# A decoder layer's projection with an interleaved paged attention: both pages' scores moved into one run, and gathered keys turned in place

## The chip, the cores and the metric

The kernel runs on one core of a Trainium2 chip. The metric is the device time of one execution in microseconds. Three runs of the kernel before gave 2318.6, 2320.21 and 2324.48 us, median 2320.21. TensorE is called PE, VectorE DVE, ScalarE ACT, GpSimd POOL and SyncE SP, as in the profile; PEld is PE's loading of weights.

## The reference

One layer is computed for a prompt of 2048 tokens and for a sample group of 8 sequences with 4 new tokens each. A normalised input is multiplied by one wide matrix (the projection); its columns feed four groups (a convolution module, a pooling mixer, stick-breaking attention, attention to memory tokens), whose gated outputs go through a second matrix. The part that the change touches is the sample group's stick-breaking attention over 8192 cached positions, kept in pages of 128 positions that a table of page numbers names:

```python
k_past = cache_k[l][page_table].reshape(bs, past, SB_HEADS, SB_HEAD_DIM)
v_past = cache_v[l][page_table].reshape(bs, past, SB_HEADS, SB_HEAD_DIM)

def sb_block(q, k, v, bias, q_pos, k_pos):
    z = (jnp.einsum('nqhd,nkhd->nhqk', q, k).astype(jnp.float32) * (SB_HEAD_DIM ** -0.5)
         + bias.astype(jnp.float32)[None, :, None, None])
    mask = (k_pos[None, :] < q_pos[:, None])[None, None]
    log_beta = jax.nn.log_sigmoid(z)
    log_1m = jnp.where(mask, jax.nn.log_sigmoid(-z), 0.0)
    rc = lax.cumsum(log_1m, axis=3, reverse=True)
    a = jnp.exp(jnp.where(mask, log_beta + rc - log_1m, -jnp.inf))
    return jnp.einsum('nhqk,nkhd->nqhd', a.astype(v.dtype), v)
```

Scores become a weight and a running product from the last position backwards, so the pages of a sequence are taken from the last to the first; the weights then sum the cached values.

## The kernel before

**The projection.** For each block of 128 output columns, `mm3` multiplies 24 pairs (high and low parts of weights and inputs) of 384, 288 or 512 token columns into one of two PSUM tiles (`z_tile`, a ring of two), called here a group. After 12 matmuls and again after the group's end it hands control back. `z_evac` then empties the tile: ACT for some column blocks, ACT's sigmoid and a multiplication on DVE for the gates (kinds cg, sg, pg, mg; names sg.. and gmg), DVE and ACT for the memory queries (mq). Tasks advance one step at each hand-back: attention to memory tokens (ms, mpt, my), the depthwise convolution on DVE (cacc, groups of two multiply-adds), transposes, stores.

**The sample part** is written as a generator, `sample_stages`, which is advanced when a running sum of the projection's work passes one; between two `yield`s stands what is issued at one hand-back. It has N = 64 stages: 2 groups of 4 sequences, 32 pairs of pages each. In a stage n:

- `load_k(n, ml)` issues on POOL one indirect gather of 128 rows of 8 KB (one page of keys for four sequences) into a tile kt; `load_v(n)` issues four gathers of 128 rows of 4 KB into tiles vt;
- `turn(n, ml)` transposes the keys of page ml in 32 by 32 blocks on DVE, in two halves of 128x1024;
- `scores(n, ml)` runs 16 fp32 products (32 matmuls in the trace) with a stationary tile of 32 columns into columns 128 ml on of the PSUM tile sSA;
- `weights(n)` takes two sigmoids of the scores (ACT; sgam and sbe), the running product (DVE scan sE) and the product sbe;
- `transposes(n)` transposes sbe on PE into the other half of sSA, ACT copies it to saT;
- `values(n)` adds the value sums of the pair, 8 fp32 products (16 matmuls in the trace), into sO, also with 32 columns.

Before the change a stage has four steps: the first page's scores and the second page's turn; the transposes of stage n - 1; the second page's scores with the value sums of n - 1, the value gathers of n, the weights of n and the first page's turn of n + 1; a step without work. Gathered keys lie in a ring of two tiles kt (`KT`), and the turned ones in one tile T (`TB`), so a turn waits until PE has read the keys turned before; each turn is followed by the gather of the next stage's page of the same parity.

**What sets the order.** The steps are put among the projection's work by `main`'s loop, and the program's framework then lays out each engine's instructions by its own planning: an instruction of DVE can stand earlier or later than in the source. Each engine works off its own row in order; PE, DVE and POOL meet at semaphores.

## Time and profile before

| | |
|---|---|
| median of three runs | 2320.21 us |
| profiled execution | 2319.3 us |
| its span | 2317.6 us |
| PE, DVE, ACT, POOL busy | 2244.9, 1704.7, 1081.0, 1261.0 us |
| granted PE clock, mean | 0.993 |
| turns on DVE (L990) | 256, 308.6 us |
| gathers of keys, of values (L957) | 128 and 256, 128.7 and 252.7 us of POOL |
| scores (L1003), value sums (L1042) | 4096 and 1024 matmuls |

The page divides the span among engines; matmul ends are modelled, so the starts of matmuls, not PE's busy share, tell how closely they follow. Waits are given as who waited for whom, with the sum, the number and the longest. The sample part's scores run from 152.7 to 1427.1 us of the span, all of it under the projection.

### The profile page before, as it was taken

Reading aid. Unit: us, or ns where it says so; the run is one execution under the profiler, and the core shown is the slowest. Engines: PE = TensorE matmul, PEld = TensorE weight load, DVE = VectorE, ACT = ScalarE, POOL = GpSimd, SP = SyncE. Lnnn points to the kernel's source line nnn. Section 1 sums busy time; section 2 is a strip of 40 time slices with the busy share of each in tenths; the row PEclk is TensorE's granted clock in tenths of the full one; section 3 lists DMA queues with packets and bytes.
Section 4 is the critical chain, followed back from the end, with each engine's and each line's share of the span. In section 5 each row is a group of like instructions: output and inputs, shape, how many; then the busy total and the mean of one; then the engine's idle time right before and its main releaser. Section 6 shows DMA issues by size and latency. Waiting matters only on the chain. (4 is left out here: it accounts for less than half of the span.)

```text
span 2317.6 us, 43407 instructions
## 1 busy us (share of the span) xinstructions
PE 2244.9 (97%) x16512; PEld 1812.9 (78%) x16512; DVE 1704.7 (74%) x2334; ACT 1081.0 (47%) x1977; POOL 1261.0 (54%) x1375
## 2 busy tenths in 40 slices
PE   7999999999999999999999999999999999999997
PEld 7998888898888777777777777667677667788775
DVE  5343786969756755378777768899989885686997
ACT  5332343242442322234233234588879875454553
POOL 3554545556464555555545455489999973620002
PEclk9999999999999999999999999999999999999999
DMA  6689977878778899987977885666554307876774
GB/s 206 208 291 316 336 259 255 286 256 277 255 252 301 306 358 338 345 284 255 319 260 259 278 275 178 160 173 192 160 161 129 98 15 217 285 236 194 251 261 152
DMA packets 338188, 558.32 MB, mean 241 GB/s; under 512 B 29162, under 2 KB 213610, under 8 KB 321580
## 3 DMA queue, kind: packets, MB, share of 16 engines
q1 hardware_dynamic: 282604, 286.83, 39.9%
q0 software_dynamic: 55376, 268.72, 32.8%
q8 instruction: 130, 2.13, 0.4%
q14 instruction: 78, 0.64, 0.1%
HBM read 465.35 MB, written 90.72 MB: 240 GB/s over the span
## 5 line engine op out<-in xcount | busy, mean ns | idle before, releaser
L990 DVE STREAM_TRANSPOSE T<-kt 128x1024 f32<-128x1024 f32 x256 | 308.6, 1226 | 183.1 <-PE sSA L1003 174.8
L957 POOL DMA_INDIRECT vt<-in_cache_v_dram,idv x256 | 252.7, 987 | 255.1 <-PE sO L1042 194.2
L642 DVE SCALAR_TENSOR_TENSOR cacc<-U,par,cacc 128x512 f32<-128x512 f32 x480 | 359.9, 750 | 11.0
L1384 POOL TENSOR_TENSOR be<-be,E 128x512 f32<-128x512 f32 (+4 forms) x316 | 311.9, 999 | 18.0 <-DVE E L1375 12.4
L957 POOL DMA_INDIRECT kt<-in_cache_k_dram,idk x128 | 128.7, 1005 | 200.2 <-DVE T L990 156.0
L1375 DVE TENSOR_TENSOR_SCAN E<-gam,cr,ZM 128x513 f32<-128x513 f32 x192 | 230.6, 1260 | 3.7 <-POOL csq L1499 1.0
L2032 PE MATMUL acc<-wohi,mh 128*128 128x512 f32 (+1 forms) x480 | 192.4, 401 | 0.0
L2032 PE MATMUL acc<-wolo,mh 128*128 128x512 f32 (+1 forms) x480 | 188.7, 393 | 0.0
L2032 PE MATMUL acc<-wohi,ml 128*128 128x512 f32 x448 | 176.9, 395 | 4.7 <-DVE ml L1767 4.7
L1405 ACT COPY at<-AT 128x512 f32<-128x512 f32 (+1 forms) x288 | 153.5, 592 | 47.9 <-PE AT L1403 42.9
L1403 PE MATMUL AT<-ident,be 128*128 128x128 f32 x1082 | 153.3, 281 | 14.6 <-ACT at L1405 10.9
L1403 PEld LDWEIGHTS AT<-ident,be 128*128 128x128 f32 x1082 | 121.2, 143 | 55.0 <-issue 22.8
L1303 ACT ACTIVATE be<-S 128x1024 f32<-128x1024 f32 (+1 forms) x158 | 153.8, 974 | 6.7 <-PE S L1298 4.1
L1415 PE MATMUL av<-at,V 128*64 128x256 f32 (+1 forms) x1152 | 137.4, 379 | 4.2 <-DVE sgt L1419 4.2
L1003 PE MATMUL sSA<-T,W 128*32 128x128 f32 x4096 | 138.3, 276 | 2.0 <-DVE T L990 1.6
L1297 PE MATMUL S<-kh,Q 128*128 128x512 f32 (+1 forms) x316 | 133.4, 426 | 1.5 <-ACT be L1303 1.5
L1003 PEld LDWEIGHTS sSA<-T,W 128*32 128x32 f32 x4096 | 104.6, 109 | 36.9 <-issue 29.0
L1415 PEld LDWEIGHTS av<-at,V 128*64 128x64 f32 x1152 | 76.6, 138 | 61.6 <-issue 23.3
L1042 PE MATMUL sO<-vt,saT 128*32 128x512 f32 x1024 | 122.4, 592 | 0.0
L1298 PE MATMUL S<-kl,Q 66*128 66x512 f32 (+1 forms) x316 | 119.5, 382 | 0.0
L1756 ACT CAST mh<-mr 128x512 fp32r<-128x512 f32 (+1 forms) x120 | 70.5, 596 | 96.5 <-PE acc L2032 26.8
L1767 DVE TENSOR_TENSOR ml<-mr,mh 128x512 fp32r<-128x512 f32 x108 | 80.6, 758 | 40.3 <-ACT mh L1756 40.0
(594 smaller groups left out, 6198.1 us busy)
## 6 DMA issues: line engine op xcount, KB each, us to landing
mr<-mixd SPq DMA_DIRECT2D x32, 512.0 KB
Q<-qd SPq DMA_DIRECT2D x96, 128.0 KB
mr<-mixd SPq DMA_DIRECT2D x48, 256.0 KB
xtp<-in_x_prompt_dram SPq DMA_DIRECT2D x16, 512.0 KB
kh<-kd SPq DMA_DIRECT2D x64, 128.0 KB
ws<-in_w_out_dram SPq DMA_DIRECT2D x16, 512.0 KB
wsd<-ws SPq DMA_DIRECT2D x16, 512.0 KB
msd<-mr SPq DMA_DIRECT2D x32, 256.0 KB
```

Of the source, the lines that this page charges most:

```text
L642: dve.scalar_tensor_tensor(out=ps, in0=U[:, a + k : a + k + H], scalar=wd[:, k : k + 1], in1=ps, op0=ALU.mult, op1=ALU.add)
L957: pool.indirect_dma_start(out=dst, out_offset=None, in_=rows, in_offset=bass.IndirectOffsetOnAxis(ap=idx, axis=0))
L990: S["turn"] = dve.transpose(T[:, 2 * hh : 2 * hh + 2].rearrange("p s j t -> p (s j t)"), kt[:, 2 * hh : 2 * hh + 2].rearrange("p s j d -> ...
L1003: pe.matmul(sSs[n][32 * g : 32 * g + 32, P * ml : P * (ml + 1)], lhsT=W[:, jj, :], rhs=T[:, :, jj, :], start=i == 0, stop=i == 3, tile_pos ...
L1297: pe.matmul(S[:, j, :w], lhsT=Q[:, 0, c], rhs=kts[0][:, :w], start=True, stop=False)
L1303: act.activation(out=be, in_=S[:, :, :w], func=AF.Sigmoid)
L1375: dve.tensor_tensor_scan(out=E[:, j][:, ::-1], data0=g_[:, j][:, ::-1], data1=ZM[:, 0:1].to_broadcast([P, 513]), initial=carry[hh, q2][:, ...
L1384: newest.append(pool.tensor_tensor(out=be[:, j, :m], in0=be[:, j, :m], in1=E[:, j, 513 - w : 513 - w + m], op=ALU.mult).ins)
L1403: pe.transpose(ap_[:, n : n + P], A[hp, qb, kc, hh, qt][:, P * r : P * (r + 1)], ident)
L1405: act.copy(at[:, :n], ap_[:, :n])
L1415: pe.matmul(av[64 * hh : 64 * hh + 64, c], lhsT=V[:, 4 * kc + r, 64 * hh : 64 * hh + 64], rhs=ats.pop((hp, qb, kc, hh, q2, r)), start=dg a ...
L2032: pe.matmul(o[:rows], lhsT=m[a][:, k, :rows], rhs=W[prod, 4 * h + k][w], start=not cont and h == k == n == 0, stop=h == 1 and k == 3 and n ...
```

## The change

Three edits belong together. The tile T is gone: a turn writes over the gathered keys in place, and the ring of kt has three tiles instead of two (the space of kt and T together is the same; the page table's tile moves into the ring). The second page's scores are joined by the first page's in one step, so that both pages' scores and the value sums of the stage before are one run of PE. And the steps are dealt anew: a step without work; scores of both pages, the second page's gather for n + 1, value sums of n - 1, value gathers, weights, the first page's turn for n + 1 and the first page's gather for n + 2; the second page's turn for n + 1; the transposes of n. One gather more is issued before the first stage, and the generator has one `yield` fewer at its end.

```diff
-TB = 1
-KT = 2
+KT = 3
...
-        ptb = sm.tile([P, NB, NPAGE], I32, tag="T", name="ptb", bufs=TB)
+        ptb = sm.tile([P, NB, NPAGE], I32, tag="kt", name="ptb", bufs=KT)
...
         def turn(n, ml):
             if n < N:
-                T = sm.tile([P, 4, 16, 32], F32, tag="T", name=f"T{n}_{ml}", bufs=TB)
-                kt = kts.pop((n, ml))
+                kt = kts.pop((n, ml)).rearrange("p s j d -> p s (j d)")
                 for hh in range(2):
-                    S["turn"] = dve.transpose(T[:, 2 * hh : 2 * hh + 2].rearrange("p s j t -> p (s j t)"),
-                                              kt[:, 2 * hh : 2 * hh + 2].rearrange("p s j d -> p (s j d)"))
-                Ts[n, ml] = T
-                load_k(n + 1, ml)
+                    half = kt[:, 2 * hh : 2 * hh + 2]
+                    S["turn"] = dve.transpose(half.rearrange("p s c -> p (s c)"), half.rearrange("p s c -> p (s c)"))
+                Ts[n, ml] = kt.rearrange("p s (j t) -> p s j t", t=32)
...
         load_v(0)
+        load_k(1, 0)
         for _ in range(Y0):
             yield
         with tc.issue_after(S["last"].ins):
             turn(0, 0)
+            turn(0, 1)
         for n in range(N):
             yield
+            yield
             scores(n, 0)
-            turn(n, 1)
-            yield
-            if n:
-                transposes(n - 1)
-                yield
-
             scores(n, 1)
+            load_k(n + 1, 1)
             if n:
                 values(n - 1)
                 load_v(n)
             weights(n)
             turn(n + 1, 0)
-            yield
+            load_k(n + 2, 0)
+            yield
+            turn(n + 1, 1)
+            yield
+            transposes(n)
         yield
-        yield
-        yield
-        transposes(N - 1)
         yield
         yield
         values(N - 1)
```

The order of the built kernels shows three places, all in stage 32, under the key columns of the projection's second half. Lines of the kernel after are 1 to 4 lower. On PE, before (sSA holds scores or transposed weights, by their inputs; z1k is the dense group, of which some rows are left out):

```order
L251 MATMUL z1k_1_8608<-xhi,wlo1k_8268 128x512
L1003 MATMUL sSA<-T_0_8577,W_1544 32x128 x16
L251 MATMUL z1k_0_8678<-xhi,whi1k_8601 128x512
...
L379 MATMUL nt1k_1_8693<-ident,zt1k_1_8643 128x128 x4
L1030 MATMUL sSA<-ident,sbe_8571 128x128 x2
L251 MATMUL z1k_0_8678<-xhi,whi1k_8601 128x512
...
L1003 MATMUL sSA<-T_1_8673,W_1544 32x128 x16
L1042 MATMUL sO_2036<-vt_0_8563,saT_8703 32x512
```

and now:

```order
L250 MATMUL z1k_1_8543<-xhi,wlo1k_8188 128x512
L1027 MATMUL sSA<-ident,sbe_8507 128x128 x2
L250 MATMUL z1k_0_8598<-xhi,whi1k_8536 128x512
...
L378 MATMUL nt1k_1_8613<-ident,zt1k_1_8580 128x128 x4
L250 MATMUL z1k_0_8598<-xhi,whi1k_8536 128x512
...
L1000 MATMUL sSA<-kt_0_8282,W_1544 32x128 x16
L1000 MATMUL sSA<-kt_1_8489,W_1544 32x128 x16
L1039 MATMUL sO_2032<-vt_0_8499,saT_8596 32x512
```

The transposes stand where the first page's scores stood, and these stand ahead of the second page's; the place between is empty.

On DVE, before (T and kt are turns, sE the scan, sbe the product of the weights, hl1k a cast of the key columns):

```order
L990 STREAM_TRANSPOSE T_0_8577<-kt_0_8345 128x1024
L1020 SCALAR_TENSOR_TENSOR sE_8574<-sgam_1564,sE_8339,zeros 128x257
L990 STREAM_TRANSPOSE T_0_8577<-kt_0_8345 128x1024
L1023 TENSOR_TENSOR sbe_8571<-sbe_8571,sE_8574 128x256
L642 SCALAR_TENSOR_TENSOR cacc_3_0_8536<-U_3_7591,par,cacc_3_0_8536 128x512
L718 CAST hl1k_1_8596<-zt1k_1_8594 128x512
L990 STREAM_TRANSPOSE T_1_8673<-kt_1_8432 128x1024
```

and now:

```order
L1017 SCALAR_TENSOR_TENSOR sE_8510<-sgam_1564,sE_8277,zeros 128x257
L1020 TENSOR_TENSOR sbe_8507<-sbe_8507,sE_8510 128x256
L989 STREAM_TRANSPOSE kt_1_8489<-kt_1_8489 128x1024 x2
L717 CAST hl1k_1_8531<-zt1k_1_8529 128x512
L717 CAST hl1k_1_8582<-zt1k_1_8580 128x512
L989 STREAM_TRANSPOSE kt_0_8515<-kt_0_8515 128x1024 x2
L1017 SCALAR_TENSOR_TENSOR sE_8697<-sgam_1562,zeros 128x257
```

The second page's turn stands directly behind the product of the weights, and no turn stands around the scan.

On POOL, before (wlo1k and hl1k are low parts of weights and of key columns):

```order
L957 DMA vt_3_8569<-in_cache_v_dram,idv 128x1024
L957 DMA kt_0_8580<-in_cache_k_dram,idk 128x2048
L719 TENSOR_TENSOR hl1k_1_8596<-zt1k_1_8594,hl1k_1_8596 128x512
L242 TENSOR_TENSOR wlo1k_8600<-wr1k_8215,whi1k_8601 128x1024
L242 TENSOR_TENSOR wlo1k_8649<-wr1k_8272,whi1k_8650 128x1024
L719 TENSOR_TENSOR hl1k_1_8645<-zt1k_1_8643,hl1k_1_8645 128x512
L957 DMA kt_1_8676<-in_cache_k_dram,idk 128x2048
```

and now:

```order
L956 DMA kt_1_8489<-in_cache_k_dram,idk 128x2048
L956 DMA vt_0_8499<-in_cache_v_dram,idv 128x1024
L956 DMA vt_1_8501<-in_cache_v_dram,idv 128x1024
L956 DMA vt_2_8503<-in_cache_v_dram,idv 128x1024
L956 DMA vt_3_8505<-in_cache_v_dram,idv 128x1024
L956 DMA kt_0_8515<-in_cache_k_dram,idk 128x2048
L718 TENSOR_TENSOR hl1k_1_8531<-zt1k_1_8529,hl1k_1_8531 128x512
```

The second page's gather, which stood alone two steps later, is the first of a burst of six.

## The prediction

> **What bounds the kernel now.** I read the page's busy times and slices first, then the sums over the stretch in which the sample part runs, 150 to 1430 us.

> ```profile
> PE 2244.9 (97%) x16512; PEld 1812.9 (78%) x16512; DVE 1704.7 (74%) x2334; ACT 1081.0 (47%) x1977; POOL 1261.0 (54%) x1375
> ...
> PE   7999999999999999999999999999999999999997
> ```
> ```profile
> 150.00:1430.00 1280.00, 1270.17 (x10683) 1033.78 (x10682) 886.50 (x1194) 423.02 (x791) 687.85 (x630) 1.00 0.84 286
> 300.00:500.00 200.00, 196.50 (x1772) 174.22 (x1771) 158.16 (x230) 76.85 (x146) 105.10 (x100) 1.00 0.77 262
> ```

> In the sums the columns are the stretch, its length, then PE, PEld, DVE, ACT and POOL. PE is idle for 1280 - 1270.17 = 9.8 us of this stretch and has the full clock. The projection there is a PE stream; whatever is cut from that stream ends the projection earlier, and all that follows moves up with it. A PE that counts as busy may still lose time between kinds of work, so the next view is the order in time around one stage's two runs (start, duration, instruction).

> ```profile
> 797.09 0.39 PE L251 MATMUL z1k<-xlo,whi1k 128*128 128x512 f32 x1
> 797.32 0.40 PE L251 MATMUL z1k<-xhi,wlo1k 128*128 128x512 f32 x1
> 797.64 1.08 PE L1003 MATMUL sSA<-T,W 128*32 128x128 f32 x32
> 798.66 0.50 PE L251 MATMUL z1k<-xhi,whi1k 128*128 128x512 f32 x1
> 798.99 0.40 PE L251 MATMUL z1k<-xlo,whi1k 128*128 128x512 f32 x1
> ...
> 805.08 1.08 PE L1003 MATMUL sSA<-T,W 128*32 128x128 f32 x32
> 805.98 1.90 PE L1042 MATMUL sO<-vt,saT 128*32 128x512 f32 x16
> ```

> Dense matmuls start 0.23 us apart (797.09, 797.32). Around a lone score run the stream stretches: from the last dense start before it (797.32) to the second after it (798.99) are 1.67 us, of which two dense steps are 0.46. **A lone score run costs 1.21 us.** Where value sums follow (both 128*32 shapes), they start 0.90 us after the scores (805.08, 805.98).

> **The term that is removed.** The first page's scores leave their own place and stand ahead of the second page's; the transposition of the weights takes the vacated place. By the row that is nearest, scores followed by the same shape, the joined run pays 0.90 instead of 1.21 us, 0.31 less. The stages are counted by this row:

> ```profile
> L1003 PE MATMUL sSA<-T,W x4096: 269/273/298, 152.7 to 1427.1; 128*32 128x128 f32 x196
> ```

> 4096 records at 64 for each stage are 64 stages, 19.9 us apart ((1427.1 - 152.7)/64). So 64 x 0.31 = **19.8 us**. Bounds: if the second page's scores follow as soon as the first's last one has started, 1.08 - 0.27 = 0.81 us, the saving is 0.40 a stage, 25.6 us; if the change of page costs as much as a change to dense work, nothing is saved. I take 19.8, since sums after scores are the same kind of seam.

> [...]

> **The turns.** Still 256 of them, in place now. The trace has no transpose in place; its row and the nearest row in place (cacc reads and writes one tile) bound it.

> ```profile
> L642 DVE SCALAR_TENSOR_TENSOR cacc<-U,par,cacc 128x512 f32<-128x512 f32 x480 | 359.9, 750 | 11.0
> L990 DVE STREAM_TRANSPOSE T<-kt 128x1024 f32<-128x1024 f32 x256 | 308.6, 1226 | 183.1 <-PE sSA L1003 174.8 <-DMA kt<-in_cache_k_dram,idk 7.9
> ```

> 1226 ns for 1024 columns is 1.20 ns each, 750 for 512 is 1.46. At the slower rate a turn takes 1.50 us, 4 x 0.27 = 1.1 us more of DVE a stage. In the stretch 300:500, ten stages, DVE works 158.16 of 200; 11 more is 169, so PE pays nothing either way. Faster than 1.20 would give PE nothing. I take 1226.

> **Waits that go, and the one that comes.** DVE's 174.8 us of waiting for the scores (one T) go, and with them POOL's wait for the turns:

> ```profile
> POOL vt L957 <- PE sO L1042: 194.2, 52, 8.5
> POOL kt L957 <- DVE T L990: 156.0, 46, 9.5
> ```

> Neither is worth anything by itself: PE's idle 9.8 us is all that they can have cost. In their place the second page's gather is issued when the first page's scores are done, in the very step of the run, while its turn stands on DVE right behind the product of the weights in 31 of 63 stages, and behind two or three conv steps of 0.75 us in 23 more (counted in the order of the built kernels). What it waits for, from the start of the joined run:

> ```profile
> DMA to landing us min/median/max: 5.6/8.1/11.7
> ```
> ```profile
> 808.13 0.96 POOL L957 DMA_INDIRECT vt<-in_cache_v_dram,idv  x1 [0.47 <-PE sO L1042]
> 809.40 0.94 POOL L957 DMA_INDIRECT vt<-in_cache_v_dram,idv  x1 [0.30 <-issue]
> ```
> ```profile
> 806.23 0.47 ACT L1014 ACTIVATE sgam<-sSA,nb 128x256 f32<-128x256 f32 x1 [0.39 <-PE sSA L1003]
> ```
> ```profile
> 826.96 0.71 DVE L1020 TENSOR_TENSOR_SCAN sE<-sgam,sE,zeros 128x257 f32<-128x257 f32 x1
> ...
> 828.73 0.38 DVE L1023 TENSOR_TENSOR sbe<-sbe,sE 128x256 f32<-128x256 f32 x1
> ```

> The gather: scores done at 1.08, POOL's start 0.47 later, landing 8.1 after that: 9.6 us. DVE: second page's scores from 0.90, the sigmoid 1.15 after their start (806.23 - 805.08) for 0.47, scan 0.71, product 0.38: 3.6 us, about 4 with the hops. So DVE stands for up to 5.6 us, and with two turns of 1.2 what is queued behind it moves from 4 to 12 us. About half the stages wait 5.6 and the rest some 3.3, 4.4 in the mean: 64 x 4.4 = 280 us, where 183 stand now. The release by PE that DVE waited for before came on time for PE by construction; this landing does not.

> **What that costs PE.** Behind the turn stand the gate multiplications and attention steps that free the two z tiles. PE covers one group: 24 dense matmuls, 4.2 us for 384 columns (0.175 each, 602.54 to 602.72 below) and 5.5 for 512. A tile filled just as DVE begins to stand is read 8 us later and costs PE up to 8 - 4.2 = 3.8 us; most fall elsewhere in the 19.9.

> ```profile
> 602.54 0.34 PE L251 MATMUL z0mq<-xlo,whi0mq 128*128 128x384 f32 x1
> 602.72 0.34 PE L251 MATMUL z0mq<-xhi,wlo0mq 128*128 128x384 f32 x1
> ```

> No row has this wait. Low end: nothing, since 183 us of DVE standing now go with 9.8 us of PE idle from all causes. High end: every fourth stage pays half of 3.8 us, 16 x 1.9 = 30 us. I take the proportion of today's row, 9.8 x 280/183 = 15.0, so **5.2 us more**; the low end is nearer, because the waits of today are of the same length and behind the same queue.

> **What is costed at nothing.** The weights' transposition now has two steps after its scores, not three: it stands where the next stage's first scores stood. The tightest such place before:

> ```profile
> 577.15 1.23 DVE L990 STREAM_TRANSPOSE T<-kt 128x1024 f32<-128x1024 f32 x1
> 578.31 0.71 DVE L1020 TENSOR_TENSOR_SCAN sE<-sgam,sE,zeros 128x257 f32<-128x257 f32 x1
> 578.93 1.22 DVE L990 STREAM_TRANSPOSE T<-kt 128x1024 f32<-128x1024 f32 x1
> 580.08 0.39 DVE L1023 TENSOR_TENSOR sbe<-sbe,sE 128x256 f32<-128x256 f32 x1
> ```
> ```profile
> 581.30 1.08 PE L1003 MATMUL sSA<-T,W 128*32 128x128 f32 x32
> ```

> The product ended at 580.47, 0.83 us ahead, after two half turns of 2.4 us that now stand elsewhere; without that relief some stages would wait a microsecond. The four value gathers start 1.25 us later behind the page (808.13, 809.40): the fifth issue at 1.6 + 5 = 6.6, landing well within the 19.9 to the next value sums; if not, PE waits for it in person. The next first page is the sixth, landing near 1.6 + 6.3 + 8.1 = 16, to be turned before the next scan at about 22. One more gather at the start, and one step fewer at the end, lie under the dense stream. SP's queue keeps its transfers.

> **The sum.** 2319.3 (profiled execution, span 2317.6) - 19.8 + 5.2 = 2304.7. The median of the runs is 0.9 above that execution: **2305 us** on that scale.

> **Rivals.** (1) *The gather hides*: DVE mostly arrives late with conv work, PE loses nothing more: 2319.3 - 19.8 + 0.9 = 2300, down to 2295 at 25.6. For it: 886.50 of 1280 us busy, so there is work to fill a wait; against: 31 stages with nothing between. [...] (2) *Half is given back*: PE pays 10 to 20 us for reads behind the turn, 2310 to 2320, within 0.3% at the upper part. (3) *The gather holds the projection*: one mechanism, a z tile unread because DVE stands at the second page's turn; it decides from 0.31 us a stage (19.8 in all), and at the high end of 30 us gives 2319.3 - 19.8 + 30 + 0.9 = 2330. For it: the gather's landing lies 5.6 us behind DVE's arrival; against: today's 183 us of like waits. [...]

> **Chances.** Forecast 0.55; (1) 0.23; (2) 0.12, half of it within 0.3%; (3) 0.06; (4) 0.04, counted with no change. A measurement of this kernel tells 0.3%, 7 us, from no change: faster (below 2313) 0.84, within 0.10, slower 0.06. The range is 2295 to 2316: the full 25.6 at its foot, half of the gain given back at its head.

> **What would show it.** After: 64 joined runs with 1.08 us scores twice in a row, the second starting 0.8 to 0.9 after the first; PE idle in the sample stretch near 15 us (right) or over 30 (rival 3); DVE's wait for T gone and a wait for the gather of 200 to 300 us; POOL's wait for the turn gone. Wrong would be: second scores 1.2 us after the first, sums of PE idle named after gates or attention steps, or a turn longer than 1.5 us.

## The result, and the profile after

| | before | after |
|---|---|---|
| median (range), six runs each | 2318.83 us (2317.3 to 2324.48) | **2378.34 us** (2363.84 to 2381.57) |
| profiled execution, its span | 2319.3, 2317.6 us | 2380.07, 2378.4 us |
| granted PE clock, mean | 0.993 | 0.981 |

The ratio is **1.024, with a 95% interval of 1.0211 to 1.0269**: slower by 2.4%, where 2305 us and faster was forecast. Of the rivals the third came nearest, with 2330.

The page of the kernel after: busy times, then PE's busy share and granted clock in 40 slices.

```profile
PE 2252.6 (95%) x16512; PEld 1836.4 (77%) x16512; DVE 1702.1 (72%) x2334; ACT 1077.2 (45%) x1975; POOL 1247.5 (52%) x1375
...
PE   7999999999979899999999999999999999999997
...
PEclk9999999999989999999999999999999999999999
```

PE has dips within the sample stretch, and the clock has one. The sums over that stretch, which now ends at 1490 instead of 1427 us (columns as in the prediction):

```profile
150.00:1490.00 1340.00, 1275.62 (x10656) 1056.15 (x10658) 876.56 (x1193) 417.67 (x787) 679.74 (x629) 0.98 0.77 273
```

PE is idle for 1340 - 1275.6 = 64.4 us, against 9.8 before. The clock is 0.98 in the mean where it was 1.00; the trace's clock records hold ten falls to one half there, 54.6 us together. 8.7 of these lie in PE's gaps, where they take nothing; in the other 45.9 PE is counted as doing half, 23.0 us, less (at the place shown below dense matmuls start 0.32 us apart where the clock is 0.50, and 0.18 where it is 1.00). After the stretch nothing changes: from the last score to the span's end are 888.2 us (2378.4 - 1490.2) and were 890.5 (2317.6 - 1427.1).

The account closes. A net length of the stretch, from 150 us to the last score, without PE's idle time and without what the clock took, is 1427.1 - 150 - 9.8 = 1267.3 us before and 1490.2 - 150 - 64.4 - 23.0 = 1252.8 us after. So the dense stream with its sample runs got 14.5 us shorter, and idle time and clock took 77.6 us more (64.4 + 23.0 - 9.8).

The waits of the kernel after (who waited for whom, sum, number, longest):

```profile
DVE kt L989 <- DMA kt<-in_cache_k_dram,idk: 277.6, 75, 8.5
POOL kt L956 <- PE sSA L1000: 182.9, 41, 13.3
...
POOL vt L956 <- PE sO L1039: 65.4, 46, 1.6
```

DVE's wait for the tile T and POOL's wait for the turn are gone, and DVE's wait for the gather is 277.6 us, against a forecast of 280. What it does to PE is seen in the order of time. DVE at one joined run (start, duration, instruction, in brackets the idle time before it and what ended it):

```profile
693.36 0.74 DVE L1017 TENSOR_TENSOR_SCAN sE<-sgam,sE,zeros 128x257 f32<-128x257 f32 x1
694.20 0.42 DVE L1020 TENSOR_TENSOR sbe<-sbe,sE 128x256 f32<-128x256 f32 x1
703.17 1.25 DVE L989 STREAM_TRANSPOSE kt<-kt 128x1024 f32<-128x1024 f32 x1 [8.54 <-DMA kt<-in_cache_k_dram,idk]
704.34 0.52 DVE L773 SCALAR_TENSOR_TENSOR mh0mq<-z0mq,mh0mq 128x384 fp32r<-128x384 f32 x1
704.78 1.22 DVE L989 STREAM_TRANSPOSE kt<-kt 128x1024 f32<-128x1024 f32 x1
```

POOL in the same place:

```profile
694.26 1.23 POOL L956 DMA_INDIRECT kt<-in_cache_k_dram,idk  x1 [0.15 <-issue]
```

And PE:

```profile
690.02 1.96 PE L1000 MATMUL sSA<-kt,W 128*32 128x128 f32 x64
691.79 1.90 PE L1039 MATMUL sO<-vt,saT 128*32 128x512 f32 x16
...
697.57 0.34 PE L250 MATMUL z0pg<-xlo,whi0pg 128*128 128x384 f32 x1
697.75 0.33 PE L250 MATMUL z0pg<-xhi,wlo0pg 128*128 128x384 f32 x1
697.92 0.40 PE L532 MATMUL ms<-mkT,mh0mq 128*128 128x256 f32 x2
704.92 1.22 PE L532 MATMUL ms<-mkT,mh0mq 128*128 128x256 f32 x4 [6.60 <-DVE mh0mq L773]
705.93 0.52 PE L250 MATMUL z0pg<-xhi,whi0pg 128*128 128x384 f32 x1
706.25 0.52 PE L250 MATMUL z0pg<-xlo,whi0pg 128*128 128x384 f32 x1
```

The product of the weights is done at 694.62. The second page's turn stands behind it, and its gather, issued at 694.26 (POOL came to it 2.3 us after the scores had ended), lets it begin at 703.17. The memory queries mh0mq stand between the two halves of the turn; PE needs them and stands for 6.60 us. Then, until 710 us, dense matmuls start 0.32 us apart instead of 0.18, under a granted clock of 0.50 (mean from 700.6 to 710.7 us; 1.00 from 690 to 700): the gap is paid a second time, in clock. The joined run does what it should: 64 score matmuls take 1.77 us to the start of the sums, 0.885 a page, here and, within 0.02 us, in each of the 63 stages with sums behind the scores (the first has none).

What this one place shows holds beyond it. Each gap of PE in the stretch can be followed back, as far as the profile names releasers: from the instruction that ended it to the one that ended that one's wait, or to the one before it on its engine. For 33.4 of the 64.4 us the way ends at the landing of a key gather (28.9 at the second page's turn, 4.5 at the first page's); in the kernel before it does so for none. PE is then mostly kept from the steps of the attention to memory tokens: of the 33.4 us, 24.2 lie ahead of ms and my, which wait for operands, and only 2.7 ahead of a group of the projection. The waits of PE for these steps, whatever the way behind them:

```profile
PE ms L532 <- DVE mh0mq L773: 7.0, 2, 6.6
PE my L558 <- DVE pL L575: 6.1, 4, 2.6
PE my L558 <- ACT pT L574: 6.1, 2, 5.4
```

### The profile page after: what moved, and what is told of

It is laid out like the page before. It is cut to its first block, busy times and chain, and to the rows that moved or that the text cites. A ratio compares the mean times of both kernels' runs of the same rounds, so it can differ in the third digit from the quotient of the medians.

```text
span 2378.4 us, 43312 instructions
## 1 busy us (share of the span) xinstructions
PE 2252.6 (95%) x16512; PEld 1836.4 (77%) x16512; DVE 1702.1 (72%) x2334; ACT 1077.2 (45%) x1975; POOL 1247.5 (52%) x1375
## 5 line engine op out<-in xcount | busy, mean ns | idle before, releaser
L989 DVE STREAM_TRANSPOSE kt<-kt 128x1024 f32<-128x1024 f32 x256 | 309.0, 1229 | 314.7 <-DMA kt<-in_cache_k_dram,idk 277.6
L1380 POOL TENSOR_TENSOR be<-be,E 128x512 f32<-128x512 f32 (+4 forms) x316 | 311.9, 998 | 19.8 <-DVE E L1371 14.7
L956 POOL DMA_INDIRECT vt<-in_cache_v_dram,idv x256 | 247.0, 965 | 129.6 <-PE sO L1039 65.4
L1399 PE MATMUL AT<-ident,be 128*128 128x128 f32 x1082 | 154.3, 282 | 16.8 <-ACT at L1401 7.5
L1000 PE MATMUL sSA<-kt,W 128*32 128x128 f32 x4096 | 125.0, 274 | 0.0
L1000 PEld LDWEIGHTS sSA<-kt,W 128*32 128x32 f32 x4096 | 108.1, 110 | 17.8 <-issue 14.0
L545 POOL TENSOR_SCALAR pr<-pr,sm 128x256 f32<-128x256 f32 x64 | 59.9, 944 | 111.9 <-DVE sm L542 97.8
L1752 ACT CAST mh<-mr 128x512 fp32r<-128x512 f32 (+1 forms) x120 | 70.6, 596 | 95.8 <-PE acc L2028 25.5
```

Of the source, the lines that this page charges most:

```text
L956: pool.indirect_dma_start(out=dst, out_offset=None, in_=rows, in_offset=bass.IndirectOffsetOnAxis(ap=idx, axis=0))
L989: S["turn"] = dve.transpose(half.rearrange("p s c -> p (s c)"), half.rearrange("p s c -> p (s c)"))
L1000: pe.matmul(sSs[n][32 * g : 32 * g + 32, P * ml : P * (ml + 1)], lhsT=W[:, jj, :], rhs=T[:, :, jj, :], start=i == 0, stop=i == 3, tile_pos ...
L1380: newest.append(pool.tensor_tensor(out=be[:, j, :m], in0=be[:, j, :m], in1=E[:, j, 513 - w : 513 - w + m], op=ALU.mult).ins)
L1399: pe.transpose(ap_[:, n : n + P], A[hp, qb, kc, hh, qt][:, P * r : P * (r + 1)], ident)
```

## The experiments

Three things recur. **Held** means that a turn gets an order edge behind the last DVE instruction that was issued before it, so that it stands on DVE where the source has it (`dve.last` is that instruction, `late` a held half turn); the planning otherwise put turns ahead of the landing of their gathers, as the runs show. **On the first page's tile** means that the second page's turn and scores take the first page's tile: every gather, turn, score and sum is still issued, but the second page's keys are left out of the result, and no turn needs a gather of its own step. **Short turns** take 32 of 1024 columns, so the turning is left out. "Loss" is PE's idle time in the sample stretch plus what the clock took there, counted as above (9.8 us before, 87.4 after); times beside "before" are of the kernel before in the same series.

### e1: no gather waits

```diff
-                kt = kts.pop((n, ml)).rearrange("p s j d -> p s (j d)")
+                kt = kts[n, 0].rearrange("p s j d -> p s (j d)")
...
-            turn(n + 1, 0)
+            with tc.issue_after(dve.last.ins):
+                turn(n + 1, 0)
```

> The changed kernel, with two edits that take DVE's waits for gathers away: the second page's turn and scores work on the first page's tile (all gathers, turns, scores and sums are still issued, so only the data of the second page is left out), and the first page's turn is held behind the weights' product, one stage after its gather. Theory (DVE stands at gathers, and PE then stands for what is queued behind): DVE's wait for kt falls from 277.6 us to under 20, PE idle between 150 and the end of the sample stretch from 64 us to about 10, no granted clock of one half there, time 2300 us (2295 to 2306), that is the joined run's 19.8 us and nothing else. Rival (turning in place, or the new dealing of steps, costs by itself): it stays above 2350, since all 256 turns and all steps are still there. Rival (the join saves nothing, and waits alone explain the loss): 2319.

Measured: 2324.65 us, before 2319.09; ratio 1.0026 (1.0001 to 1.0051). The sums of e1 over its sample stretch:

```profile
150.00:1435.00 1285.00, 1257.39 (x10668) 1043.19 (x10670) 891.30 (x1193) 416.86 (x787) 683.31 (x629) 0.99 0.81 285
```

Who waited for whom in e1:

```profile
ACT zt0v L746 <- DMA out_dram<-nat0k: 8.5, 1, 8.5
...
DVE kt L1008 <- DMA kt<-in_cache_k_dram,idk: 4.5, 1, 4.5
```

54 us of the 59.5 are gone with the waits, although all 256 turns in place and all the new steps are still there: the rival that these cost by themselves falls. (The hold also moves the first page's turn in DVE's order; e12 asks what that does alone.) But 2300 is not reached. PE idle is 27.6 us, the loss 33.2. One gap of 7.8 us is at the start: a copy of the value columns waits for its buffer's store (the first row of the waits), and the clock behind it, 0.72 in the mean from 180 to 190 us, takes 2.2 more. The kernel after has the same gap with 4.51 us. That is 10 us; of the loss some 13 above the 9.8 of before are left to explain.

### e2, e14, e3, e4: whose wait counts

e2 holds the first page's turn, e14 the second page's (issued in the step of the transposes), e3 both, and e4 both with the second one a step later still. The edits, e2's and then that of e14:

```diff
-            turn(n + 1, 0)
+            with tc.issue_after(dve.last.ins):
+                turn(n + 1, 0)
...
-            turn(n + 1, 1)
             yield
             transposes(n)
+            with tc.issue_after(dve.last.ins):
+                turn(n + 1, 1)
```

That there are two waits came from matching the trace's 256 transposes, in their order, with the rows of the built kernel: of the 277.6 us in the kernel after, 151.8 stand at the **first** page's turn and 125.8 at the second's. The first page's gather is the sixth of the burst, and the planning had put its turn between the second page's and the next scan, up to a stage before the source has it. PE's gaps, however, lie beside waits for the second page (31 of 64 us) much more than beside the first page's (5.8).

> The changed kernel with one edit: the first page's turn of stage n + 1 is held on DVE behind the weights' product of stage n (the source has it there, but the planning put it up to a stage earlier, in front of its own gather, the sixth of the burst). Its 151.8 us of waiting go. Theory (both pages' waits add up on DVE, whichever page it is): the second page's turn is met 2.4 us later behind two half turns, so its 125.8 us fall to 40 to 70; PE idle falls from 64 to 15 to 35 us, time 2305 to 2335. Rival (only the second page's wait matters, since but 5.8 us of PE's idle time lie beside the first page's): 2355 to 2375. Rival (turning in place costs by itself): 2378.

> The changed kernel with the second page's turn alone held on DVE until the step of the weights' transposes; the first page's turn stays where the planning puts it. Holding the first page's alone gave 2348.36 us, holding both 2328.1. Theory (the second page's wait is the one beside which PE stands: 31 of 64 us): its 125.8 us of waiting fall to 30 to 60, the first page's 151.8 stay at 100 to 150 or grow, 2335 to 2352. Rival (only the sum of the waits counts): with a sum near 180 us 2350 to 2362.

> As the run before, and the second page's turn too is held: it is issued in the step of the weights' transposes, two steps after the joined run instead of one, behind the DVE work issued until then. Theory: DVE's wait for kt falls below 60 us, PE idle to 10 to 20 us, time 2300 to 2312. Rival (a turn in place or the new dealing of steps costs by itself): 2350 or more. Rival (a later second turn makes PE wait for the turned keys): the waits of PE for kt rise from nearly nothing, 2320 to 2340.

> As the run before, with the second page's turn one step later still: in the first step of the next stage, one step ahead of the joined run that reads it. Theory: DVE's wait for kt below 25 us, PE idle near 10 us, time 2298 to 2308. Rival (the turn is now late for the scores): PE waits for kt in person, 2320 to 2345. Rival (in place or steps by themselves): 2350 or more.

| | wait for kt, us | first + second page | loss | time | before |
|---|---|---|---|---|---|
| after | 277.6 | 152 + 126 | 87.4 | 2378.34 | 2318.83 |
| e14, second held | 249.3 | 172 + 77 | 57.6 | 2351.23 | 2322.14 |
| e2, first held | 108.9 | 4 + 105 | 58.5 | 2348.36 | 2319.09 |
| e3, both held | 60.0 | 5 + 55 | 37.4 | 2328.10 | 2319.09 |
| e4, both, later | 47.0 | 3 + 44 | 41.7 | 2334.28 | 2319.09 |

Holding either page's turn gains about 30 us, both about 50, so both waits count. That only the second page's would count, as the gaps beside the waits had suggested, falls with e2. That a wait delays DVE as a whole, and PE then stands later and at some other name, is the likely reason, but it is argued: e2 moves the turn too. By the expectations e14 went by its theory, e2 was slower than its theory and faster than its rivals, and e3 (2300 to 2312) fell within the range of its second rival, though not by that rival's cause: PE has no wait for kt there. Nor is the sum of the waits the price: e14 takes away 28 us of them and gains as much as e2 with 169. e4 went by its rival: the turn comes too late for its own reader, and PE waits in person, as e4's waits show:

```profile
DVE kt L1008 <- DMA kt<-in_cache_k_dram,idk: 47.0, 24, 5.3
PE sSA L1019 <- DVE kt L1008: 10.8, 8, 2.9
```

### e5, e6: four pieces instead of a block

The four half turns of a stage go into four steps, each held; e5 on the first page's tile, e6 with the real keys.

```diff
+            if n:
+                late(n, 1, 1)
             yield
             scores(n, 0)
...
-            turn(n + 1, 0)
+            late(n + 1, 0, 0)
             load_k(n + 2, 0)
             yield
-            turn(n + 1, 1)
+            late(n + 1, 0, 1)
             yield
             transposes(n)
+            late(n + 1, 1, 0)
```

> As the run without gather waits (the second page's data left out again), and the four half turns of a stage, which stood there as one block of 4.6 us on DVE, are issued in four different steps, each behind the DVE work issued until then. That run left 27.4 us of PE idle and three falls of the granted clock, 2324.65 us. Theory (the block is a wait too: what frees PE's tiles stands 4.6 us behind turns in one piece): PE idle falls to 10 to 15 us, time 2300 to 2310. Rival (the rest comes from the start, where a copy waits for a store, 7.8 us at 173): that gap stays and the others go, 2308 to 2316. Rival (the new dealing of steps or turning in place costs by itself): no change, 2320 to 2330.

> The same spreading with the keys of both pages as they should be, so the second page's two half turns come two and three steps after the joined run that frees their tile. Theory (late and in four pieces, the gather has landed and no block stands): DVE's wait for kt under 40 us, PE idle 10 to 20 us, time 2302 to 2314. Rival (the last half comes too late for the joined run): PE waits for kt in person for 10 us and more, 2320 to 2335, as when both were held three steps (2334.28).

Measured: 2341.25 and 2339.35 us, before 2319.97. Both are slower than with the block. In e5 DVE's wait for kt is 16.8 us, but PE now waits for the last half: 19.5 us of its 38.0 us idle stand ahead of scores. The waits of e5:

```profile
PE sSA L1023 <- issue: 19.5, 8, 4.8
...
DVE kt L1008 <- DMA kt<-in_cache_k_dram,idk: 16.8, 4, 7.5
```

The first row names no releaser, but in each of the eight places the last half turn ends 0.1 us before PE starts. So e5 doesn't test the block: it brought in another wait. e6 went by its rival (13.3 us of PE waiting for kt), some 4 us above that rival's range; its wait of DVE for kt is 112.8 us, where under 40 was expected.

### e7, e11, e12, e10: the runs apart

e7 keeps the turns in place and the ring of three but puts the two score runs back in their places of before, with the first page's turn held. e11 holds the second page's turn too. e12 is the kernel before with both turns held. e10 is e11 with short turns. The steps of e7:

```diff
-            yield
             scores(n, 0)
+            load_k(n + 1, 1)
+            turn(n, 1)
+            yield
+            if n:
+                transposes(n - 1)
+                yield
+
             scores(n, 1)
-            load_k(n + 1, 1)
```

> Only the turns in place and the ring of three are kept; the two score runs stand in their two places as before the change, so a gather is issued a whole stage ahead of its turn, and the first page's turn is held behind the weights' product. Theory (in place costs nothing; what costs is the gather next to its turn): DVE's wait for kt below 30 us, PE idle near 10 us, time 2314 to 2325, as before the change. Rival (in place, or three tiles, cost by themselves): 2340 to 2380.

> As e7_in_place_apart (2370.8 us, where the planning had put the second page's turn a stage early, in front of its own gather: 212 us of waiting), but now the second page's turn is held on DVE too until its step, a stage after its gather. Full turns of both pages. Theory (the gather next to its turn is the cost; in place costs nothing): DVE's wait for kt under 20 us, PE idle 10 to 20, 2316 to 2328. Rival (in place or the ring of three costs by itself): stays above 2345.

> The kernel before the change, with one edit: both turns are held on DVE behind the work issued until their step, so DVE's order is another while its waits for gathers stay near nothing (7.9 us before). It asks what another order alone does. Theory (gather waits alone explain the loss): 2316 to 2323, PE idle near 10 us. Rival (the order of before is good by itself, any other one puts some gate late): PE idle 15 to 30 us with one to three falls of the clock, 2325 to 2340.

| | wait for kt | loss | time | before |
|---|---|---|---|---|
| e7 | 215.6 | 53.3 | 2370.80 | 2319.97 |
| e11 | 48.7 | 31.4 | 2346.25 | 2320.77 |
| e12 | 3.0 | 24.0 | 2335.29 | 2320.77 |

e7 was to have no waits, and its time lies in the range of its rival; but the planning put the second page's turn a stage early, in front of its own gather, and without any join the kernel lost 51 us. Holding it there gives half of that back. e12 was the surprise: the kernel before, its tile T and all, loses 14.5 us when its turns merely stand elsewhere in DVE's order, without gather waits (3.0 us). The order of DVE in the kernel before is better than the one that holding makes; the part of e1 that was left can be the same, since e1 holds a turn too, but no run shows that it is. Of e11's 25.5 us, 14.5 can be that as well; its turns take 1220 ns as e12's take 1221. By its time, just above 2345, e11 went to its rival, that turning in place or the ring of three costs by itself. Its condition, waits under 20 us, was not met (48.7), and e12, which turns into T from a ring of two, already has 24.0 of e11's 31.4 us of loss: some 7 us are left for that rival, if the two orders cost alike. The turns of e11, grouped by line (busy time and mean ns, then the idle time before them and what ended it):

```profile
L1008 DVE STREAM_TRANSPOSE kt<-kt 128x1024 f32<-128x1024 f32 x256 | 303.1, 1220 | 51.7 <-DMA kt<-in_cache_k_dram,idk 48.7 <-issue 3.0
```

The same group of e12:

```profile
L1009 DVE STREAM_TRANSPOSE T<-kt 128x1024 f32<-128x1024 f32 x256 | 303.1, 1221 | 96.9 <-PE sSA L1022 89.0 <-remote 4.8 <-DMA kt<-in_cache_k_dram,idk 3.0
```

In e12 DVE still stands 89.0 us for PE, and 3.0 for gathers; in e11 it is 48.7 for gathers.

### e9 and e10, e9 and e15: the join and the wait, each by itself

All three have short turns; e9 is e1, e10 is e11, e15 is the kernel after.

```diff
-                    half = kt[:, 2 * hh : 2 * hh + 2]
-                    S["turn"] = dve.transpose(half.rearrange("p s c -> p (s c)"), half.rearrange("p s c -> p (s c)"))
+                    half = kt[:, 2 * hh, 0:32]
+                    S["turn"] = dve.transpose(half, half)
```

> The joined run without gather waits, as in the first experiment (second page's data left out), and each turn now takes 32 of its 1024 columns (the turning is left out), so DVE has some 280 us less to do. That experiment came to 2324.65 us with 27.4 us of PE idle. Theory (what stayed there is lateness of DVE, the join's 19.8 us are real): PE idle about 10 us, no half clock, 2295 to 2304. Rival (the joined run itself does not save PE time): equal within 5 us to the next run.

> The same short turns (the turning is left out), turned in place in the ring of three, but the two score runs stand apart in their places of before; both turns are held on DVE until their step. It has the same work as the run before but for the join. Theory: 15 to 26 us slower than it, by the 19.8 us of 64 lone runs, that is 2312 to 2325. [...]

> The changed kernel with all its gathers and waits, but each turn takes 32 of its 1024 columns (the turning is left out), so DVE has some 280 us less to do. Without the waits the same short turns gave 2307.54 us. Theory (standing at a gather is what costs, whatever DVE's load): DVE's wait for kt 300 us or more, since it comes earlier to it, PE idle 30 to 50 us, 2335 to 2365. Rival (DVE's load is the cost and the wait only fills spare time): 2305 to 2320.

Measured: e9 2307.54 (ratio 0.9946, 0.992 to 0.9972), e10 2324.20, before 2320.77; e15 2346.72, before 2322.14. e10 is 16.7 us slower than e9, as its theory had it. The two do not wait alike (DVE's wait for kt is 71.4 us in e10, 3.1 in e9), but with the loss taken off (e9 18.0, with the gap at the start, e10 14.0) the net lengths are 1249.4 and 1270.3. Over all kernels of this study the net length is 1248.5 to 1254.4 us in the thirteen joined ones, mean 1251.2, and 1267.3 to 1273.8 in the five with the runs apart, mean 1270.2. **The join saves 19 us**, and no joined kernel comes near one with the runs apart.

e15 differs from e9 by its waits, 405.4 us against 3.1, and by the hold of the first page's turn, which e9 has. It is 39 us slower, with a loss of 59.3 against 18.0. The waits of e15, then of e9:

```profile
DVE kt L989 <- DMA kt<-in_cache_k_dram,idk: 405.4, 97, 12.1
```
```profile
DVE kt L1008 <- DMA kt<-in_cache_k_dram,idk: 3.1, 1, 3.1
```

So waits cost even where DVE has little to do; the rival that its load is the whole cost falls. But the load counts too. Against the kernel after, e15's DVE has 247 us less to do (1455.2 against 1702.1 us busy), and the loss falls from 87.4 to 59.3 us although the waits grow by 128.

### e8, e13, e16: what the planning answers

e8 puts the second page's gather behind the value gathers in the source; e16 does so with an order edge on POOL; e13 is e1 without the hold.

```diff
-            load_k(n + 1, 1)
...
                 load_v(n)
+            with tc.issue_after(S["lv"].ins):
+                load_k(n + 1, 1)
```

(e16; in e8 without the `with`.)

> The changed kernel with one line moved: the second page's gather is issued behind the four value gathers instead of ahead of them, so it lands some 5 to 6 us later, and nothing else changes. Theory: DVE's wait for kt grows from 278 to 430 us or more, nearly all of it at the second page's turn, PE idle grows from 64 to over 120 us, with more time at half clock, time 2440 to 2620. Rival (the waits are only a sign, and something else in the change costs): within 20 us of 2378.

> The second page's turn and scores work on the first page's tile (its data left out; all work is issued), and nothing is held: DVE's order is the planning's own. Gathers run a stage ahead, since nobody reads every second tile. Theory (gather waits cost, and in the first experiment holding the turns cost the rest): DVE's wait for kt under 40 us, PE idle 10 to 18 us, 2298 to 2310. Rival (something else in the joined version costs, whatever the order): 2320 to 2330 as in the first experiment.

> The changed kernel with the second page's gather held on POOL behind the four value gathers; the planning answers by putting its turn later on DVE (right behind the product in 8 stages instead of 29, 11 or more instructions behind it in 30). Theory (a wait costs by what stands behind it; the planning counts on a landing that is some 5 us too early wherever the gather stands): DVE's wait for kt stays above 200 us, 2355 to 2400. Rival (the later place hides the landing): wait under 150 us, 2325 to 2350.

e8: 2376.11 us in a single run. In the built kernel the second page's gather still stands ahead of the four others: the planning had put it back. In its trace DVE, POOL, ACT and PE work off the same instructions in the same order as in the kernel after. So it tells nothing of the gather's place, but how much one order scatters: its wait is 310.2 us against 277.6, and its loss 79.8 against 87.4. The 28 us that e14 took away lie within that scatter of the wait, its gain of 30 us does not.

e13: 2383.77 us, before 2322.14. Its theory fell on its premise. With every second tile free at once the gathers run ahead, and the planning put all four half turns further ahead too, again in front of a gather, as its waits show:

```profile
DVE kt L989 <- DMA kt<-in_cache_k_dram,idk: 212.0, 43, 15.6
```

e16: 2431.97 us, before 2322.14, slower than its theory had it. DVE's wait is 295.0 us, longest 15.2, and PE now waits for the turned keys as well. The waits of e16:

```profile
DVE kt L989 <- DMA kt<-in_cache_k_dram,idk: 295.0, 78, 15.2
...
PE sSA L1000 <- DVE kt L989: 42.3, 23, 7.3
```

e1, e13 and e16 together: wherever the gather stood in these runs, the planning's own order put the turn in front of its landing; only a hold kept the two apart.

No version with all its work beats the kernel before. The best joined one is e3, 2328.1 us (ratio 1.0045, 1.0026 to 1.0064).

## Why the prediction was wrong, point by point

- **The bound.** Right: what PE is kept from, and nothing else, sets the time. Net length, idle time and clock give 2317.6 - 14.5 + 54.6 + 23.0 = 2380.7 for the span of the kernel after; it is 2378.4, as the rest behind the stretch is 2.3 shorter.
- **The term removed, 19.8 us.** Right, 19 by the thirteen and five kernels (14.5 between before and after alone). A score run inside costs 0.885 us where the forecast had 0.90, and (1.21 - 0.885) x 64 = 20.8. That nothing would be saved, the last of the chances with 0.04, falls.
- **The turns in place, 1226 ns.** Right, 1229.
- **DVE's wait for the gather, 280 us.** The sum is right, 277.6, but by chance: 64 waits of 4.4 us at the second page's turn were meant; 37 waits and 125.8 us stand there, 38 waits and 151.8 us at the first page's.
- **"The next first page is the sixth, landing near 1.6 + 6.3 + 8.1 = 16, to be turned before the next scan at about 22"**, costed at nothing: wrong. The landing was set against the time of the scan, and not against where DVE's order has the turn. In the trace DVE comes to it 17.2 us after the run's start in the median (9.6 to 22.9), and the gather, issued at 9.1 instead of 7.9, lands at about the same time. Holding the first page's turn alone gained 30 us (e2).
- **The step that failed: "I take the proportion of today's row, 9.8 x 280/183 = 15.0", from which the 5.2 us more came.** The price was 54.6 us of idle time, and the high end, 30, fell short too. Waits of the same length behind the same queue were taken to cost alike. Those of before ended when PE had finished a score run (174.8 of the 183.1 us); those of after end when a transfer lands (277.6 us), whatever PE needs meanwhile. The prediction says so itself one paragraph earlier and then prices them as equal. The high end had only unread z tiles in view, with a group's 4.2 us as cover; most of what can be followed back went through operands of the attention to memory tokens (24.2 of 33.4 us). That turns standing ahead of a landing are the main cause is shown: by these 33.4 us, and by e1 and e3, which win back 54 and 50 us with the joined run and all turns in place. That the older waits were cheap because PE ended them is argued, since no run changed only that.
- **The clock, missing from the sum.** With no fall in the stretch before, none was priced: it took 23.0 us, to 54.6 of idle time.
- **What else was costed at nothing.** The value gathers were: PE waits for none. The transposes a step earlier nearly so: PE waits 5.6 us for the product, in two places, the longer one (3.98 us) behind a gather wait. The start was not: 4.51 us at 174, and 3.41 us of half clock behind it. The gap is 7.8 us in e1, 6.0 in e9 and 3.3 in e13, and at most 1.1 in e2 to e6; what decides it is open.
- **DVE's order itself.** No step had it. e12 shows that another order, without gather waits, costs 14.5 us. How much of the 60 us is order and how much waiting can't be split finer than that: every edit that took a wait away also moved instructions.
- **The rivals and the chances.** The third rival, given 0.06, had the right direction and the right cause, DVE standing at a gather, though not the way to PE (a z tile) and only one of the two turns. Its own condition, "it decides from 0.31 us a stage", was met nearly four times over: the loss grew by 77.6 us, 1.21 a stage.

## What to carry to other kernels

When a DVE wait changes its releaser from the engine that is the bound to a transfer, price it anew: take what stands behind it on that queue, and ask for each who waits for it, not for what share of older waits was paid. Read the place of a moved instruction from the built order and put each transfer's landing beside that place, for every gather of the burst; a planner may put the reader ahead of the landing, as it did for both pages here. And add to PE's gaps what the clock may take behind them: in the kernel after ten of the 14 gaps of 1.75 us and more had half clock behind them, and it took 23.0 us.
